# Splitting the first eight tiles of a fused LoRA kernel into parts of one and seven

## The chip, the cores and the metric

The kernel runs on one core of a Trainium2 chip. The metric is device time in microseconds (us) of one execution; the kernel before takes 124.86 us, the median of three runs (124.82 to 125.03). A profile, taken in an execution of its own, shows what each engine and each DMA queue did in it.

## The reference

A low-rank update is added to every row of x:

```python
"x": (16, 512, 768) f32, "A": (768, 16) f32, "B": (16, 768) f32, "scale": 0.5
lora = np.matmul(np.matmul(x, A), B)
return (x + scale * lora).astype(np.float32)
```

That is 8192 rows of 768 floats. They are read once and written once, 25.2 MB each way; A and B are 48 KB each.

## The kernel before

The 8192 rows are cut into 64 tiles of 128 rows, one row of a tile on each of the 128 partitions; a tile is 384 KB, 3 KB on each partition. Tiles are gathered in parts (`PARTS`, line 14): 8, 8, 16, 16 and 16 tiles. In a part of S tiles, partition p holds S rows that follow one another in memory (`memory`, line 88), so that a transfer of the whole part moves one piece of S x 3 KB for each partition. `LOADS` (line 98) and `STORES` (line 120) list the transfers as (part, first tile, tiles). The first part is read in two pieces, 2 tiles and then 6, the last in two of 8; the others in one. Every part is stored in one piece but the last, stored in two. The buffer `x_all` has room for 48 tiles (`ROOM`, line 57), so that the last 16 tiles are read into the places of the first 16, once these are stored.

The work runs in 8 groups of 8 tiles (`GROUP`, `NG`), two halves of 4 tiles in each. For each half ScalarE or GpSimd casts the x tiles to f16 (`narrowed`, line 168, the copy is L178), VectorE transposes them in 32x32 blocks (`turned`, L235), TensorE multiplies with A, which was laid out in blocks beforehand (`projected`, L263). ScalarE scales the small product and lays it out (L222), TensorE multiplies with B (`raised`, L280), for two tiles at a time, and VectorE adds the result to x in place (`summed`, L240). The addition that ends a group which is the last of a store raises the semaphore `s_sum`.

Every DMA is issued by SyncE (SP), on one queue, in an order written out by hand in `on_sync` (line 127): loads 0 and 1; A (L143) and B (L147), each after a memset by GpSimd; loads 2, 3 and 4. Then SP waits for the first low-rank product, issues store 0 as soon as the first group is added and store 1 as the second is (`store`, line 132, the wait at L133, the issue L138). Then it waits until store 0 has landed (line 159) and issues load 5, and for store 1 (line 161) and issues load 6; both fill places that these stores have emptied. At last it issues stores 2 to 5, each as its groups are added. A transfer of 128 partitions is spread over the core's 16 DMA engines; its completion adds up to 16 on a semaphore. `narrowed` waits for each load that its four tiles touch; for tiles 0 to 3 these are loads 0 and 1. GpSimd waits at the end (line 314) for the last four stores. `store` also gives TensorE the last `s_free` of a group, which on other groups the addition gives itself.

Of the kernel before, what the change touches and what calls it, by code (L numbers as in the profile page):

```python
# [10 lines left out]

PARTS = [8, 8, 16, 16, 16]


GROUP = 8
# [7 lines left out]
def kernel(  # L25
# [8 lines left out]
    nc = tc.nc  # L34
# [9 lines left out]
    NC = D // 64  # L44
    NG = sum(PARTS) // GROUP
    PAIRS = GROUP // 2
    assert sum(PARTS) * P == T and NG * GROUP == sum(PARTS)
    sc = float(scale)


    def sb(name, shape, dtype):
        return nc.alloc_sbuf_tensor(name, shape, dtype).ap()
# [3 lines left out]

    ROOM = sum(PARTS[:-1])
    x_all = sb("x_sb", [P, ROOM, D], fp32)
# [17 lines left out]
    def sem(name):  # L76
        return tc.alloc_semaphore(name)
# [3 lines left out]
    where = []  # L81
    tok = 0
    for i, S in enumerate(PARTS):
        parts.append(tok)
# [3 lines left out]
    def memory(t2, i, s, n):  # L88
        S = PARTS[i]
        return t2[ds(parts[i], S * P), :].rearrange("(p s) d -> p s d", s=S)[:, ds(s, n), :]  # L90

    def held(i, s, n):
        return tiles(where.index((i, s)), n)

    def tiles(t, n):
        return x_all[:, ds(t % ROOM, n), :]

    LOADS = [
        (0, 0, 2), (0, 2, 6), (1, 0, 8), (2, 0, 16), (3, 0, 16), (4, 0, 8), (4, 8, 8)
    ]  # L100
    s_load = [sem(f"s_load{k}") for k in range(len(LOADS))]

# [12 lines left out]
    s_free = [sem(f"s_free{p}") for p in range(PAIRS)]  # L115
    s_sum = sem("s_sum")
    s_out0, s_out1, s_out = sem("s_out0"), sem("s_out1"), sem("s_out")

    MMS = 2 * NC
    STORES = [(0, 0, 8), (1, 0, 8), (2, 0, 16), (3, 0, 16), (4, 0, 8), (4, 8, 8)]  # L120

    STORED = [where.index((i, s + n - 1)) // GROUP for i, s, n in STORES]

    section = ExitStack()
    section.enter_context(tc.tile_critical(no_gpsimd_drain=True))  # L125
# [1 line left out]
    def on_sync(e):  # L127
        def load(k):
            ld = LOADS[k]
            e.dma_start(out=held(*ld), in_=memory(x2, *ld)).then_inc(s_load[k], 16)  # L130

        def store(k, done):
            st = STORES[k]  # L133
            e.wait_ge(s_sum, k + 1)
            if STORED[k] + 1 < NG:

                e.sem_inc(s_free[PAIRS - 1], 1)
            e.dma_start(out=memory(out2, *st), in_=held(*st)).then_inc(done, 16)  # L138

        load(0)  # L140
        load(1)
        e.wait_ge(s_ready, 1)
        e.dma_start(  # L143
            out=a_rows[0 : NC * APART : APART, :], in_=A.rearrange("(c e) r -> c (e r)", e=64)
        ).then_inc(s_a, 16)
        e.wait_ge(s_brows, 1)
        e.dma_start(out=b_rows[0 : R * APART : APART, :], in_=B).then_inc(s_b, 16)  # L147
        for k in range(2, len(LOADS) - 2):
            load(k)

        e.sem_inc(s_spread, 1)
        for p, n in ((0, 1), (2, 2), (3, 2)):
            e.sem_inc(s_free[p], n)

        e.wait_ge(s_lora, 1)
        e.sem_inc(s_free[1], 1)
        store(0, s_out0)
        store(1, s_out1)
        e.wait_ge(s_out0, 16)
        load(len(LOADS) - 2)  # L160
        e.wait_ge(s_out1, 16)
        load(len(LOADS) - 1)
        for k in range(2, len(STORES)):
            store(k, s_out)

    here = set()
# [58 lines left out]
    def on_vector(e):  # L225
# [11 lines left out]
        def summed(g, p):  # L237
            xs = tiles(g * GROUP + 2 * p, 2)
            e.wait_ge(s_lora, (g + 1) * PAIRS + p + 1)
            ins = e.tensor_tensor(out=xs, in0=xs, in1=lora[p % 2], op=mybir.AluOpType.add)  # L240
            if p + 1 == PAIRS and g in STORED:
                ins.then_inc(s_sum, 1)
# [12 lines left out]
    def on_tensor(e):  # L255
# [49 lines left out]
        for p in range(PAIRS):  # L305
            raised(p)

    on_sync(nc.sync)
    on_gpsimd(nc.gpsimd)
    on_scalar(nc.scalar)  # L310
    on_vector(nc.vector)
    on_tensor(nc.tensor)

    nc.gpsimd.wait_ge(s_out, (len(STORES) - 2) * 16)
    section.close()


# [33 lines left out]
```

## Time and profile before

| what | before |
|---|---|
| median of 3 runs | 124.86 us |
| profiled execution, its own time | 125.2 us |
| span of that execution | 123.4 us |
| busy: TensorE, VectorE, ScalarE, GpSimd | 58.3, 82.5, 38.7, 27.3 us |
| DMA | 50.43 MB in 1928 packets, 409 GB/s over the span |
| load 0 (768 KB) from issue to landing | 4.7 us |
| load 1 (2304 KB) from issue to landing | 10.4 us |
| store 0 (3072 KB): issue, time to landing | 36.38 us, 19.4 us |
| last addition ends, last store is issued | 105.8 us |

The span goes from the first to the last instruction of the profiled execution; the profiled execution's own time is 1.8 us longer, and lies 0.34 us above the median. A packet is one contiguous piece that one DMA engine moved; a packet of 4 bytes at the end of a transfer on each engine raises its semaphore. "Busy" is the time in which an engine executes; "landing" is the time at which a transfer's semaphore is full.

### The profile page before, as it was taken

How to read it: one execution, taken by the hardware profiler on the slowest of the kernel's cores; microseconds unless marked ns; L12 is line 12 of the kernel's file. 1: busy time of each engine (PE TensorE's matmuls, PEld its weight loads, DVE VectorE, ACT ScalarE, POOL GpSimd, SP SyncE). 2: the span in 40 equal slices, each digit the busy share in tenths (PEclk: the TensorE clock that was granted, in tenths of full speed). 3: DMA queues.
4: the chain of work that ended last, by engine and by line, in shares of the span. 5: the costliest groups of instructions: out<-in, count | busy, mean ns of one | idle time of the engine just before them, and what ended most of it. 6: DMA issues, size and time to landing. Idle time of an engine off the chain costs nothing.

```text
span 123.4 us, 1313 instructions
## 1 busy us (share of the span) xinstructions
PE 58.3 (47%) x530; PEld 39.2 (32%) x530; DVE 82.5 (67%) x49; ACT 38.7 (31%) x43; POOL 27.3 (22%) x25
## 2 busy tenths in 40 slices
PE   0000249948565994844854775576484452000000
PEld 0000028736352862523614534255253311000000
DVE  0000555059985999999999999999999889200000
ACT  0001992760094085264083072353400400000000
POOL 7500660071035008005203501700800000000000
PEclk9999999999855599999999999999999999555555
DMA  3999996997999898999999999899989989899980
GB/s 66 422 430 372 430 574 287 510 478 335 462 494 398 382 510 358 398 446 430 430 454 390 446 446 502 382 414 478 462 351 478 446 382 446 382 446 414 438 366 8
DMA packets 1928, 50.43 MB, mean 409 GB/s; under 512 B 236, under 2 KB 236, under 8 KB 392
## 3 DMA queue, kind: packets, MB, share of 16 engines
q1 hardware_dynamic: 1928, 50.43, 96.1%
HBM read 25.26 MB, written 25.17 MB: 409 GB/s over the span
## 4 chain that ended last, share of the span: by engine, by line
DVE 54%; PE 13%; DMA 8%; ACT 5%; issue 4%; SPq 0%; ACTq 0%
DVE x_sb L240 38%; DVE xh L235 16%; DMA x_sb<-in_x_dram 8%; PE ps_yt L263 7%; PE lora_ps L280 6%; ACT xh L178 2%; ACT y_bd L222 1%; ACT L178 1%; ACT b_mm L214 1%; SPq L130 0%; SPq L346 0%; SPq L125 0%; ACTq L173 0%
## 5 line engine op out<-in xcount | busy, mean ns | idle before, releaser
L240 DVE TENSOR_TENSOR x_sb<-x_sb,lora_ps 128x1536 f32<-128x1536 f32 x32 | 54.1, 1732 | 3.2 <-PE lora_ps L280 3.2
L280 PE MATMUL lora_ps<-b_mm,y_bd 128*128 128x512 f16 (+1 forms) x144 | 30.6, 352 | 24.2 <-ACT y_bd L222 10.0
L178 ACT CAST xh<-x_sb 128x3072 f16<-128x3072 f32 x9 | 24.8, 2752 | 29.4 <-PE ps_yt L263 22.3
L235 DVE STREAM_TRANSPOSE xh<-xh 128x1536 f32<-128x1536 f32 x16 | 28.2, 1765 | 8.0 <-ACT xh L178 8.0
L263 PE MATMUL ps_yt<-xh,w_bd 128*128 128x128 f16 x384 | 28.2, 235 | 7.5 <-DVE xh L235 7.5
L178 POOL CAST xh<-x_sb 128x3072 f16<-128x3072 f32 x7 | 19.2, 2746 | 52.6 <-PE ps_yt L263 52.6
L263 PEld LDWEIGHTS ps_yt<-xh,w_bd 128*128 128x128 f16 x384 | 26.0, 105 | 12.7 <-issue 12.3
L280 PEld LDWEIGHTS lora_ps<-b_mm,y_bd 128*128 128x128 f16 x144 | 13.1, 103 | 37.7 <-issue 20.9
L222 ACT ACTIVATE y_bd<-ps_yt 32x256 f16<-32x256 f32 x32 | 12.0, 374 | 18.1 <-PE ps_yt L263 17.8
L227 DVE STREAM_TRANSPOSE a_t<-a_rows 96x1024 f32<-96x1024 f32 x1 | 1.9, 1930 | 12.1 <-DMA a_rows<-in_A_dram 12.1
L292 PE MATMUL lora_ps<-b_half,pick 128*128 128x512 f16 (+1 forms) x2 | 0.8, 504 | 13.4 <-POOL b_half L194 13.4
L178 ACT ACT_TABLE_LOAD x1 | 1.3, 1283 | 11.9 <-DMA x_sb<-in_x_dram 11.9
L292 PEld LDWEIGHTS lora_ps<-b_half,pick 128*128 128x128 f16 x2 | 0.1, 103 | 13.4 <-issue 13.4
L194 POOL CAST b_half<-b_rows 128x768 f16<-128x768 f32 x1 | 0.8, 822 | 7.6 <-DMA b_rows<-in_B_dram 7.6
L204 POOL COPY w_bd<-w_one 32x384 f16<-32x384 f16 x4 | 2.0, 500 | 0.2
L198 POOL CAST w_one<-a_t 32x128 f16<-32x128 f32 x3 | 1.2, 390 | 1.0 <-DVE a_t L227 0.8
L185 POOL MEMSET w_bd<- 128x1536 f32 x1 | 1.4, 1378 | 0.0
L182 POOL MEMSET a_rows<- 96x1024 f32 x1 | 0.9, 948 | 0.5 <-SPq L125 0.5
L214 ACT CAST b_mm<-lora_ps 128x768 f16<-128x768 f32 x1 | 0.8, 798 | 0.0
L183 POOL MEMSET b_rows<- 128x768 f32 x1 | 0.7, 734 | 0.0
L186 POOL MEMSET y_bd<- 128x512 f32 x1 | 0.5, 522 | 0.0
L188 POOL TENSOR_SCALAR_AFFINE_SELECT pick<-pick 128x128 f16<-128x128 f16 x1 | 0.3, 306 | 0.0
(5 smaller groups left out, 0.6 us busy)
## 6 DMA issues: line engine op xcount, KB each, us to landing
x_sb<-in_x_dram SPq DMA_DIRECT2D x2, 6144.0 KB, 36.8
out_dram<-x_sb SPq DMA_DIRECT2D x4, 3072.0 KB, 16.5
out_dram<-x_sb SPq DMA_DIRECT2D x2, 6144.0 KB, 22.0
x_sb<-in_x_dram SPq DMA_DIRECT2D x3, 3072.0 KB, 14.7
x_sb<-in_x_dram SPq DMA_DIRECT2D x1, 2304.0 KB, 10.4
x_sb<-in_x_dram SPq DMA_DIRECT2D x1, 768.0 KB, 4.7
a_rows<-in_A_dram SPq DMA_DIRECT2D x1, 48.0 KB
b_rows<-in_B_dram SPq DMA_DIRECT2D x1, 48.0 KB, 9.4
```

The source lines that it names most:

```text
L178: last = copy(out=xh[h][:, ds(k, n), :], in_=tiles(t + k, n))
L182: e.memset(a_rows[0 : NC * APART], 0.0).then_inc(s_ready, 1)
L185: e.memset(w_bd.rearrange("p c k m -> p (c k m)").bitcast(fp32), 0.0)
L198: e.tensor_copy(out=w_one[:, ds(b * EACH, EACH), :, :], in_=a_t[ds(b * Q, Q)].rearrange("i k r (c n) -> i c k r n", n=APART)[..., 0],).the ...
L204: e.tensor_copy(out=w_bd[ds(b * Q, Q), :, :, ds(b * Q, R)], in_=w_one).then_inc(s_w, 1)
L214: e.copy(out=b_mm, in_=lora[0][:, 0, :]).then_inc(s_bm, 1)
L222: last = e.mul(out=y_bd[q, :, q], in_=y_ps[q, :, :], mul=sc)
L227: e.transpose(out=a_t[0 : NC * APART].rearrange("i k r c -> i (k r) c"), in_=a_rows[0 : NC * APART].rearrange("c (i k r) -> c (k r) i", k= ...
L235: e.transpose(out=v, in_=v).then_inc(s_turned[h], 1)
L240: ins = e.tensor_tensor(out=xs, in0=xs, in1=lora[p % 2], op=mybir.AluOpType.add)
L263: mm = e.matmul(y_ps[:, ds(h * SUB, SUB), :], w_bd[:, c, k, :], xv[:, :, c, :, k], start=(m == 0), stop=(m == MMS - 1),)
L280: mms.append(e.matmul(t[:, k, ds(n0, w)], y_bd[:, 2 * p + k, :], b_mm[:, ds(n0, w)], start=True, stop=True,))
```

## The change

The first 8 tiles become two parts, of 1 and of 7 tiles, each read in one transfer. The part of 7 is stored first, right behind it the 1, both after the first group's additions; both count up `s_out0`, and load 5 waits for the 32 of both. `store` waits on `s_sum`, and gives `s_free`, only for the first store that ends in a group. The memory rows that a partition holds change with it: one row of the first 128, and 7 that follow one another of the next 896. In memory, the first load went over pieces of 6 KB that are 24 KB apart, the second over pieces of 18 KB; now they are pieces of 3 KB and of 21 KB that follow one another. The number of transfers goes from 15 to 16.

```diff
-PARTS = [8, 8, 16, 16, 16]
+PARTS = [1, 7, 8, 16, 16, 16]
...
     LOADS = [
-        (0, 0, 2), (0, 2, 6), (1, 0, 8), (2, 0, 16), (3, 0, 16), (4, 0, 8), (4, 8, 8)
+        (0, 0, 1), (1, 0, 7), (2, 0, 8), (3, 0, 16), (4, 0, 16), (5, 0, 8), (5, 8, 8)
     ]
...
-    STORES = [(0, 0, 8), (1, 0, 8), (2, 0, 16), (3, 0, 16), (4, 0, 8), (4, 8, 8)]
-
-    STORED = [where.index((i, s + n - 1)) // GROUP for i, s, n in STORES]
+    STORES = [(1, 0, 7), (0, 0, 1), (2, 0, 8), (3, 0, 16), (4, 0, 16), (5, 0, 8), (5, 8, 8)]
+
+    ENDED = [where.index((i, s + n - 1)) // GROUP for i, s, n in STORES]
+    STORED = list(dict.fromkeys(ENDED))
...
         def store(k, done):
             st = STORES[k]
-            e.wait_ge(s_sum, k + 1)
-            if STORED[k] + 1 < NG:
-
-                e.sem_inc(s_free[PAIRS - 1], 1)
+            if k == 0 or ENDED[k] != ENDED[k - 1]:
+                e.wait_ge(s_sum, STORED.index(ENDED[k]) + 1)
+                if ENDED[k] + 1 < NG:
+
+                    e.sem_inc(s_free[PAIRS - 1], 1)
             e.dma_start(out=memory(out2, *st), in_=held(*st)).then_inc(done, 16)
...
         store(0, s_out0)
-        store(1, s_out1)
-        e.wait_ge(s_out0, 16)
+        store(1, s_out0)
+        store(2, s_out1)
+        e.wait_ge(s_out0, 32)
         load(len(LOADS) - 2)
         e.wait_ge(s_out1, 16)
         load(len(LOADS) - 1)
-        for k in range(2, len(STORES)):
+        for k in range(3, len(STORES)):
             store(k, s_out)
...
-    nc.gpsimd.wait_ge(s_out, (len(STORES) - 2) * 16)
+    nc.gpsimd.wait_ge(s_out, (len(STORES) - 3) * 16)
```

## The prediction

> **What bounds the kernel now.** I read the page from the DMA rows outward, because the list of costly groups alone would point to VectorE: DVE is busy 67% of the span, and the chain that ended last is 54% DVE.
>
> ```profile
> DMA  3999996997999898999999999899989989899980
> q1 hardware_dynamic: 1928, 50.43, 96.1%
> DVE 54%; PE 13%; DMA 8%; ACT 5%; issue 4%; SPq 0%; ACTq 0%
> ```
>
> The first row is the share of the 16 DMA engines in use, in 40 slices: full from the second slice to the last but one. The second says that one queue moved 50.43 MB and that its packets took 96.1% of 16 engines' span. The chain's shares add up to 84%, and in order of time it stops with VectorE's last addition at 105.8 us, while the span ends at 123.4; what fills the rest is the stores. The DMA view cut to 12 to 120 us settles it:
>
> ```profile
> DMA packets 1543, 46.50 MB, mean 431 GB/s; under 512 B 163, under 2 KB 163, under 8 KB 163
> q1 hardware_dynamic: 1543, 46.50, 100.0%
> ```
>
> 100.0% for 108 us: the queue never runs dry. So the kernel lasts as long as its packets do, plus about 2 us before the first (share 0.06 in the windows view from 0 to 2 us) and about 3 us behind the last (0.06 from 120 to 122). A second question is whether SP always issues the next transfer before the queue is empty. The timeline of SP (start us, duration us, line) gives the issues:
>
> ```profile
> 0.97 0.85 SPq L130 DMA_DIRECT2D x_sb<-in_x_dram  x2
> 3.47 1.74 SPq L130 DMA_DIRECT2D x_sb<-in_x_dram  x3
> 36.38 12.33 SPq L138 DMA_DIRECT2D out_dram<-x_sb  x2
> 55.78 7.63 SPq L130 DMA_DIRECT2D x_sb<-in_x_dram  x2
> 68.33 37.83 SPq L138 DMA_DIRECT2D out_dram<-x_sb  x4
> ```
>
> A merged row covers several issues; asked one by one, the DMA view gives each one's time to landing. The last early load lands at 48.4 (issued near 4.7, 43.7 later, the longest landing), and store 0 was issued at 36.38: 12.0 us of cover. Store 0 lands at 55.8 (19.4 after issue), store 1 at 63.1 (48.38 + 14.7), the two late loads at 70.4 and 77.8 (55.78 + 14.6, 63.07 + 14.7), the next stores at 92.8 (68.33 + 24.5), 107.7 (88.27 + 19.4), 114.9 (98.25 + 16.7) and 122.2 (105.83 + 16.4). Each issue against the landing ahead of it: cover of 7.3 us for both late loads, 9.5 for the store at 68.33, 4.5 at 88.27, 9.5 at 98.25, 9.1 at 105.83. The smallest is 4.5 us.
>
> **The change part by part.** Compute first: the order of instructions on PE, DVE, ACT and POOL stays as it was; only SP gets one DMA more.
>
> *Price of a packet.* The trace's records of single packets have one length for each size, nearly without exception: 3 KB (3072 B) 121 ns, 6 KB 234, 18 KB 686, 24 KB 912, 48 KB 1815. From 24 to 48 KB it is 903 ns for 24,576 B, 36.7 ns per 1000 B, which leaves about 8 ns per packet; 3072 B by that line are 121, as seen, and 21 KB (21,504 B) come to 799. A completion packet of 4 B takes 9 ns. Each transfer of 128 rows is 8 packets on each of 16 engines.
>
> *The two first loads.* Before: 8 x 234 + 8 x 686 = 7.36 us on each engine. After: 8 x 121 + 8 x 799 = 7.36 us. Nothing. ScalarE's first cast takes tiles 0 to 3, which span both loads before and after, so its start (table load at 11.88, on load 1, issued at 1.35 with 10.4 to landing) stays; that load 0 alone lands sooner helps nobody. If the first load is now so short that the second is not ready behind it, a gap opens: the first's packets began 1.0 us after its issue (0.97 to 1.97) and 1.7 us after it at the latest (2.65); the second is issued at 1.35, so ready from 2.4 to 3.1; the first now needs 0.97 us of packets, and the very first of each engine was some 0.5 us longer than 234 ns. It ends at 2.9 at the earliest and mostly after 3.3. No gap.
>
> *The first stores.* Before: 8 x 912 + 9 = 7.31 us. After, 8 x 799 + 9 and 8 x 121 + 9 = 7.38 us: **+0.07 us**, in a full queue, so it reaches the end whole. SP's own issue of the second store (0.34 us) comes right behind the first, at 36.7, and next on SP is the wait for the second group at 48.4: 11 us of cover.
>
> *The wait for both stores.* Load 5 now waits for two completions in one semaphore. They come 0.07 us later than the one of before; queued behind that wait on SP are load 6 and the stores from 68.33 on, all with at least 4.5 us of cover. If that cover were gone, the same 0.07 us would be paid once more.
>
> *Order.* POOL's last wait counts the same four stores. The 1 and 7 tiles lie where the 8 lay, so the wrap of the last 16 tiles onto the first stays.
>
> *Unknown: 3 KB packets in a row.* No row shows eight in a row, nor a store of 3 KB. Nearest are the 16 of 3 KB that load B: 11 at 121 to 133 ns, the others up to 219, mean 141. So one 1-tile transfer costs between nothing and 8 x 98 ns = 0.78 us more than the line says, 0.16 at the mean. And behind the two small loads of A and B the first 24 KB packet on most engines took near 1340 ns for 912: a stall of **0.43 us**, where the completions came 0.13 to 0.17 us apart. Behind load 0 (1.9 us of packets) load 1's first packets were mostly 686, no stall. A 1-tile transfer lies between, 0.97 us from completion to completion. Its nearest row is that of load 0: half as long, against a seventh. I take no stall and the line's 121 ns; both upper ends go to the range.
>
> *Below nothing.* Load 0's packets took 328 ns in the mean for 234: 8 x 94 = 0.75 us on each engine are lost as the traffic starts. If that went with the bytes of the first load, half would go: -0.37 us. Much of it is the first packet's own wait, though, which stays.
>
> *A rule that speaks against the change.* The Trainium skill, "DMA: Bandwidth & Descriptors", section "Anatomy of one DMA — SWDGE (gpsimd) path", gives a DMA (measured on those that GpSimd issues) a fixed cost of about 2.0 us, mostly the receipt of the last write; by that an added DMA would cost an estimated 2 us if nothing hid it, 126.9 us in all. Here store 1 lands 7.3 us behind store 0 and its packets alone take 7.3: the next transfer runs under the receipt.
>
> *Sum.* The profiled execution took 125.2 us, its span 123.4. With +0.07 it is 125.27; the median of the runs, 124.86, is 0.34 lower, so **124.93 us**. A measurement of this kernel tells about 0.2% (0.25 us) from no change, and this is 0.06%.
>
> **The rivals.**
>
> *Short transfers stall the queue (slower).* Place: the 1-tile store and the packet behind it. It decides if completions 0.97 us apart are still too close. Price: the 0.43 us stall of A and B, with 0.16 us for each of the two 3 KB transfers at B's mean: +0.50 to +0.82 in all, 125.4 to 125.7 us. For it: the stall stands in the trace. Against: it came with gaps of 0.17 us, and a stall that makes up a fixed delay (0.17 + 0.43 = 0.6 us) would be over after 0.97. With every 3 KB packet at its worst, and a stall behind both, it is +2.5 us, 127.4; this needs the worst of 16 packets 16 times running.
>
> *The start loses less (faster).* Half of load 0's 0.75 us goes: 124.56 us. For it: the lost time is spread over several packets of an engine, not only its first. Against: load 1 then is the one to start, with more packets left in the slow stretch.
>
> *A fixed cost shows (slower).* If the added store had its own start and receipt in the open, it would cost the 1.0 us from issue to first packet and some 0.4 us from last packet to landing: 126.3 us. Against: 100.0% from 12 to 120 us over 8 such seams.
>
> *It does not do what it says.* Were the 128 rows of the 1-tile part joined into fewer, longer packets, as they lie in one piece in memory, the time would be that of before, 124.86. The 8-tile part, in one piece too, was 128 packets of 24 KB, so I expect 128 of 3 KB.
>
> **How the numbers follow.** Forecast, with the joined rows: 0.57, from 124.75 to 125.1. Stall 0.25. Less lost at the start 0.15. Fixed cost 0.03. So faster by over 0.2% 0.15, within 0.2% 0.57, slower 0.28. The range reaches over the first two rivals: low 124.55, high 125.7; left out are the fixed cost, the worst packets, and what lies below the half of the start.
>
> **What would show it.** Small packets: under 8 KB from 392 to near 536 (128 of 3 KB in the store, 16 completions; the first load's 128 stay under 8 KB). From 12 to 120 us still 100.0%. The seven tiles land some 1 us before the one; the wait ahead of load 5 ends at 55.8 to 55.9. Last addition still at 105.8, last store's landing at 122.3. Wrong would be: a first 24 KB packet behind the 1-tile store well above 912 ns, 3 KB packets well above 121, or a DMA share under 9 tenths near 55 us.

## The result and the profile after

The changed kernel is slower: 125.28 us median (124.97 to 126.52, 22 runs) against 124.96 (124.72 to 125.43, 22 runs), a ratio of 1.0042 with an interval of 1.0026 to 1.0058. Measured twice more it came to 1.0021 (1.0007 to 1.0035) and 1.0032 (1.0015 to 1.0050). The medians lie 0.30 to 0.33 us apart in all three; the first ratio is larger because 8 of its 22 runs took more than 125.55 us. Two runs of e2 below (126.91 and 127.13 us) lie over 1.5% above the fastest of their kernel and are left out of its median and ratio.

The rows of the page of the changed kernel that answer to those shown of before, in the same order:

```profile
DMA  3999999899799697999999999799899989899980
q1 hardware_dynamic: 2072, 50.43, 96.3%
DVE 50%; DMA 24%; ACT 5%; PE 3%; SPq 2%; POOL 1%; issue 1%; POOLq 0%
```

2072 packets for 1928, as many more as eight on each engine and one more completion make. The queue is still full, and between 12 and 120 us, by the DMA view, its share is 100.2%:

```profile
DMA packets 1683, 46.38 MB, mean 429 GB/s; under 512 B 180, under 2 KB 180, under 8 KB 308
q1 hardware_dynamic: 1683, 46.38, 100.2%
```

SP issues as planned (start us, duration us, line), three stores merged in the row at 34.25, the late loads at 55.79:

```profile
0.97 0.86 SPq L131 DMA_DIRECT2D x_sb<-in_x_dram  x2
3.47 1.59 SPq L131 DMA_DIRECT2D x_sb<-in_x_dram  x3
34.25 13.90 SPq L140 DMA_DIRECT2D out_dram<-x_sb  x3
55.79 7.66 SPq L131 DMA_DIRECT2D x_sb<-in_x_dram  x2
67.77 37.84 SPq L140 DMA_DIRECT2D out_dram<-x_sb  x4
```

So nothing ran dry, and yet some time went. Where it went is seen when a window's GB/s is divided by its DMA share. Both count a packet where it begins, so the quotient is the rate of the packets while they run. These are the windows of the first profile of before (columns: window, its length, busy time and number of instructions of PE, PEld, DVE, ACT and POOL, granted clock, DMA share, GB/s):

```profile
12.00:44.00 32.00, 21.76 (x166) 15.57 (x167) 21.58 (x13) 16.20 (x15) 9.48 (x10) 0.84 1.03 444
44.00:50.00 6.00, 3.93 (x38) 2.40 (x35) 6.00 (x5) 3.92 (x5) 2.75 (x1) 1.00 0.85 365
50.00:74.00 24.00, 15.46 (x160) 10.25 (x160) 24.00 (x15) 10.80 (x11) 5.49 (x2) 1.00 1.01 434
```

and of the changed kernel in its third profile (run e9_after_third below):

```profile
12.00:44.00 32.00, 20.65 (x178) 14.59 (x179) 22.23 (x14) 17.10 (x15) 8.94 (x10) 0.95 1.02 442
44.00:50.00 6.00, 4.01 (x52) 3.02 (x48) 6.00 (x5) 2.17 (x5) 2.75 (x1) 1.00 0.90 325
50.00:74.00 24.00, 14.62 (x148) 9.40 (x147) 24.00 (x16) 11.26 (x11) 5.50 (x2) 1.00 1.01 433
```

Before: 444/1.03 = 431, 365/0.85 = 429, 434/1.01 = 430. Changed: 433, then 325/0.90 = 361, then 429. From 44 to 50 us the early loads end and the first stores begin; I call it **the seam**. The DMA engines there are busy but move a sixth less. In the first profile of the changed kernel it is less marked, 353/0.90 = 392:

```profile
44.00:50.00 6.00, 3.84 (x43) 2.59 (x42) 6.00 (x5) 3.39 (x5) 2.75 (x1) 1.00 0.90 353
```

The records of single packets show which packets are slow: the last 48 KB packet of load 4 on every engine, 2.3 to 2.9 us long in that third profile for 1.815.

The gain ahead of it shows in the time to landing of load 1 in the DMA view, the last column. Before:

```profile
x_sb<-in_x_dram SPq DMA_DIRECT2D x1, 2304.0 KB, 10.4
...
x_sb<-in_x_dram SPq DMA_DIRECT2D x1, 6144.0 KB, 43.7
```

Changed, third profile:

```profile
x_sb<-in_x_dram SPq DMA_DIRECT2D x1, 2688.0 KB, 9.6
...
x_sb<-in_x_dram SPq DMA_DIRECT2D x1, 6144.0 KB, 43.6
```

Load 1 lands 0.8 us sooner after an issue at the same time, load 4 (6144 KB) no longer does. These are the last of 16 engines. The engine in the middle (median of the 16 completions) scatters less; its landings, as means of two profiles of before and three of the changed kernel, in us:

| landing | before | changed | difference |
|---|---|---|---|
| load 1 | 10.88 | 10.44 | -0.44 |
| load 3 | 33.22 | 32.74 | -0.48 |
| load 4 | 47.78 | 47.93 | +0.16 |
| first store or stores | 55.07 | 55.28 | +0.21 |
| last store | 120.49 | 120.78 | +0.29 |

In these means half a microsecond is gained at the start, 0.64 us is lost between load 3 and load 4, and 0.13 us behind it. The last row is as large as the difference of the medians of the runs (+0.30 to +0.33), but it can't be taken as its proof, for two reasons. The landing of load 4 differs less between the kernels than within them: 47.88 and 47.68 before, 47.75, 48.08 and 47.97 changed. And an execution ends with its last engine, not with the middle one: its time is some 3.0 us more than the last landing of the last store in every profile (3.1 in e6). That landing came at 122.20 and 121.88 before and at 121.98, 122.31 and 122.21 changed, 0.13 us later in the mean; the five executions themselves took 125.20 and 124.87, and 124.98, 125.30 and 125.20 us, also 0.13 us apart. The loss at the seam is there in every profile of the changed kernel; that it is what makes up the 0.3 us of the medians is not shown by so few profiles.

### The profile page after: what moved, and what is told of

It reads as the page before. It is cut to its first block, busy times and chain, and to the rows that moved or that the text cites. A ratio compares the mean times of both kernels' runs of the same rounds, so it can differ in the third digit from the quotient of the medians.

```text
span 123.2 us, 1314 instructions
## 1 busy us (share of the span) xinstructions
PE 55.6 (45%) x530; PEld 36.9 (30%) x530; DVE 82.5 (67%) x49; ACT 38.7 (31%) x43; POOL 27.3 (22%) x25
## 2 busy tenths in 40 slices
DMA packets 2072, 50.43 MB, mean 409 GB/s; under 512 B 252, under 2 KB 252, under 8 KB 536
## 3 DMA queue, kind: packets, MB, share of 16 engines
q1 hardware_dynamic: 2072, 50.43, 96.3%
## 4 chain that ended last, share of the span: by engine, by line
DVE 50%; DMA 24%; ACT 5%; PE 3%; SPq 2%; POOL 1%; issue 1%; POOLq 0%
DVE x_sb L243 35%; DMA x_sb<-in_x_dram 24%; DVE xh L238 15%; ACT y_bd L225 2%; ACT xh L181 2%; PE lora_ps L283 2%; PE ps_yt L266 1%; POOL a_rows L185 1%; SPq L145 1%; SPq L131 0%; SPq L149 0%; POOLq L349 0%; SPq L126 0%
## 5 line engine op out<-in xcount | busy, mean ns | idle before, releaser
L283 PE MATMUL lora_ps<-b_mm,y_bd 128*128 128x512 f16 (+1 forms) x144 | 30.1, 348 | 26.9 <-ACT y_bd L225 15.3
L266 PE MATMUL ps_yt<-xh,w_bd 128*128 128x128 f16 x384 | 25.9, 224 | 7.4 <-DVE xh L238 7.4
L266 PEld LDWEIGHTS ps_yt<-xh,w_bd 128*128 128x128 f16 x384 | 23.9, 99 | 12.7 <-issue 12.3
```

Of the source, the lines that this page charges most:

```text
L266: mm = e.matmul(y_ps[:, ds(h * SUB, SUB), :], w_bd[:, c, k, :], xv[:, :, c, :, k], start=(m == 0), stop=(m == MMS - 1),)
L283: mms.append(e.matmul(t[:, k, ds(n0, w)], y_bd[:, 2 * p + k, :], b_mm[:, ds(n0, w)], start=True, stop=True,))
```

## The experiments

In the profiles I read three numbers besides the time: the landing of load 3 on the middle engine; the loss at the seam, which is the length of all packets that begin from 40 to 48 us beyond the usual length of their size, divided by 16 engines; and the time from load 4's landing to that of the stores of the first eight tiles. Load 3 and load 4 are in every kernel the two early loads of 16 tiles; in e11 and e12, where the second is cut in two, the landing is that of its second piece. The diffs show only the changed part of a long line.

| kernel | load 3 us | seam loss us | load 4 us | first stores us |
|---|---|---|---|---|
| before, first profile | 33.34 | 0.02 | 47.88 | 7.27 |
| before again, e4 | 33.11 | 0.09 | 47.68 | 7.33 |
| e8, stores 6, 1, 1 | 33.07 | 0.16 | 47.68 | 7.38 |
| e2, loads 1, 7 alone | 32.95 | 0.39 | 47.73 | 7.30 |
| e3, stores 7, 1 alone | 32.95 | 0.42 | 47.77 | 7.33 |
| changed, first profile | 32.87 | 0.49 | 47.75 | 7.35 |
| e6, one load of 8 | 32.83 | 0.47 | 47.69 | 7.33 |
| e1, changed | 32.72 | 0.92 | 48.08 | 7.35 |
| e7, one tile stored first | 32.72 | 0.77 | 47.92 | 7.35 |
| e10, the same | 32.65 | 0.84 | 47.87 | 7.36 |
| e9, changed | 32.64 | 0.90 | 47.97 | 7.35 |
| e11, changed, late store | 32.74 | 0.05 | 47.35 | 7.32 |
| e12, before, late store | 33.29 | 0.05 | 47.89 | 7.28 |
| e5, changed, store held | 32.57 | 0.01 | 47.10 | - |

**e1: the changed kernel again** (no edit).

> The changed kernel as it is, to see which of its lost time comes back. In its first profile every engine's last 48 KB packet of load 4 (the packets that began at 45.0 to 45.7 us) took 2.0 to 2.5 us for 1.815, about 0.5 us lost per engine at the seam from loads to stores; before had nothing there. Theory S (the added store upsets that seam, now that two stores are queued behind the loads): the stretch of about 0.5 us is there again, median 1.002 to 1.006 of before. Theory N (the seam's stretch is a chance of that one execution): under 0.1 us this time, and the runs scatter from 124.9 to 126.5 for a reason that the seam doesn't show.

125.24 us against 124.91; seam loss 0.92. The stretch of the last packets was there again, and larger, so theory N falls for the changed kernel. Its window gives 314/0.87 = 361 GB/s at the seam:

```profile
44.00:50.00 6.00, 3.83 (x47) 2.97 (x48) 6.00 (x5) 1.93 (x5) 2.75 (x1) 1.00 0.87 314
```

**e2: only the loads.**

```diff
-        (0, 0, 2), (0, 2, 6), (1, 0, 8),
+        (0, 0, 1), (0, 1, 7), (1, 0, 8),
```

> Parts and stores as before; the first part is read as 1 and 7 tiles in place of 2 and 6. Only the sizes of the first two loads change. Theory S: the loss came from the store, so this is no slower than before, 0.996 to 1.001 (load 1 lands up to 0.6 us sooner, as it did in the changed kernel: 11.2 for 11.8 us). Theory L (3 KB packets at the start are what scatters): slower by 0.2 to 0.6%, with single runs up to 126.5.

124.98 us against 124.91, ratio 1.0018 (0.9995 to 1.0040). Not clear of no change. The stretch is there (0.39) without any added store, so theory S, that the added store makes it, falls. Theory L, that small first packets scatter the runs, is neither shown nor excluded by this interval.

**e3: only the stores** (the changed `store`, with parts and loads of before).

```diff
-    STORES = [(0, 0, 8), (1, 0, 8),
+    STORES = [(0, 1, 7), (0, 0, 1), (1, 0, 8),
```

> Parts and loads as before; the first part is stored as 7 tiles and then 1, with rows of 21 KB and 3 KB that lie 24 KB apart in memory. One store more than before. Theory S: the whole loss, 1.002 to 1.006 of before, with the stretch before the first store in the profile. Theory L: no loss, 1.000 to 1.001. If both parts alone are within 0.1% of before, it is the layout: rows of 3 KB and 21 KB that follow one another.

125.09 us, 1.0011 (0.9997 to 1.0025), seam loss 0.42. Inconclusive in time: the halves alone come to +0.07 and +0.18 us in the median and neither is clear of nothing. The stretch came with either half, in one profile each. But the loads of e3 are those of before, and here load 3 landed at 32.95 for 33.11 and 33.34: so early an arrival, with the stretch, does not need the new loads.

**e4: before again** (no edit).

> The kernel before as it is, for a second profile of it. Theory S: no stretch at the seam from loads to the first store (last 48 KB packets near 1815 ns, as in the first profile). Theory N: the stretch comes and goes here too, anything from 0 to 0.5 us.

124.87 us, seam loss 0.09, most of it on the three engines that came first to the seam. As theory S had it for before; but with e2 beside it, what goes with the loss is not the added store. In the table it goes with the landing of load 3: the sooner the loads come, the more is lost, and load 4 lands at 47.7 to 48.1 whatever was gained. I formed two theories from that: the turn (T: loads with a store queued behind them are held) and the early arrival by itself (A).

**e5: no store in the queue behind the loads.**

```diff
+        e.wait_ge(s_load[len(LOADS) - 3], 16)
         store(0, s_out0)
```

> The changed kernel, in which SP waits for the last early load (load 4, about 47.7 to 48.1 us) before it issues the first store: no store stands queued behind the loads. The queue runs dry for 1 to 2 us there, which is the price of looking. Theory T (the turn: the last 48 KB packets of load 4 are held because a store follows them in the queue): they take about 1.815 us, no more than 0.1 us lost per engine before 48 us, where three profiles of changed kernels lost 0.39 to 0.92. Theory A (the engines arrive at the end of the loads early and together, whatever follows): the stretch of 0.3 to 0.9 us stays.

129.91 us, seam loss 0.01, load 4 lands at 47.10, 0.87 us ahead of e9. As T had it. But the price was far above the queue's dry spell, for a reason that I had overlooked: `store` also hands TensorE the buffer of the next group, behind my wait. VectorE stood for 8.5 us at just that time (lines are shifted by one in this kernel):

```profile
49.50 1.75 DVE L244 TENSOR_TENSOR x_sb<-x_sb,lora_ps 128x1536 f32<-128x1536 f32 x1 [8.46 <-PE lora_ps L284]
```

So it also fits a third theory, C: the sums that run beside the transfers hold them.

**e6: one first load of 8 tiles** (so `load(1)` and the loop behind it move up by one).

```diff
-        (0, 0, 2), (0, 2, 6), (1, 0, 8),
+        (0, 0, 8), (1, 0, 8),
```

> The kernel before with its first part read in one transfer of 8 tiles: packets of 24 KB from the start, one transfer less. Theory of the first load's size (smaller first packets lose less at the start, and the seam takes it back): loss per engine before 9.5 us at least that of before, 0.7 to 0.8 us (3 KB first packets: 0.36 to 0.64), and little stretch at the seam, below 0.2 us; time 0.999 to 1.002 of before. Rival: the start's loss does not follow the size of the first packets; then it is anywhere from 0.3 to 0.8.

124.95 us, 1.0010 (0.9999 to 1.0022). The start lost 0.69 us (before 0.69 and 0.78), as expected; the seam 0.47, which I had put below 0.2. It stands in its place in the table by the landing of load 3, not by the size of its first packets.

**e7: the one tile stored first.**

```diff
-    STORES = [(1, 0, 7), (0, 0, 1),
+    STORES = [(0, 0, 1), (1, 0, 7),
```

> The changed kernel with the one tile stored ahead of the seven: the 3 KB packets then come right at the seam from loads to stores, where eight small packets leave little in flight. If the order matters, 0.1 to 0.5 us slower or faster than the changed kernel (125.24); if it is only the number of packets and the reading at the start, the same within 0.1 us: 1.002 to 1.003 of before.

124.94 us, 1.0004 (0.9993 to 1.0016). Its eight small packets on each engine took 121 ns each, right at the seam. The time is below the changed kernel's 125.24 of e1, so I ran both side by side (e10). With a seam loss of 0.77 it is not clear of before here: the loss at the seam alone does not tell how slow a kernel is.

**e8: two stores more** (the changed `store`, parts and loads of before; 48 in the wait for `s_out0`).

```diff
-    STORES = [(0, 0, 8), (1, 0, 8),
+    STORES = [(0, 2, 6), (0, 0, 1), (0, 1, 1), (1, 0, 8),
```

> Loads and parts as before; the first part is stored as 6 tiles, then 1, then 1: two stores more than before, where the kernel with stores of 7 and 1 had one more and came to 125.09 against 124.91. If an added store costs what its packets do (0.07 us), this is +0.15 us, 125.05. If each added store costs 0.18 us as that run's median seemed to say, +0.36 us, 125.27. The landing of the last of the three small stores, seen from the landing of load 4, tells it with less scatter: 7.3 us before, +0.07 or +0.18 for each.

124.88 us, 1.0003 (0.9993 to 1.0013). The first stores took 7.38 us: one store 7.27 to 7.33 in the four profiles above (before, e4, e2, e6), mean 7.30; two 7.33 to 7.36, mean 7.35; three 7.38. So an added store costs some 0.04 us, and not 0.18.

**e9: the changed kernel a third time** (no edit), **and e10: e7 again**, on one chip.

> The changed kernel once more, beside the two below on one chip: 1.002 to 1.004 of before, loss at the seam before 48 us 0.4 to 0.9 us, load 1 landing near 10.4 us (median of the engines).

> The changed kernel with the one tile stored ahead of the seven, a second time, now beside the changed kernel itself. It came to 1.0004 of before, though its profile showed the same early start and the same stretch at the seam (0.77 us) as the changed kernel. If the order of the two stores matters, it is again below the changed kernel by 0.1 to 0.4 us. If that was scatter between calls, the two are within 0.1 us of each other.

e9: 125.20 us, 1.0032 (1.0015 to 1.0050); e10: 125.06 us, 1.0020 (1.0002 to 1.0038). Seam losses 0.90 and 0.84. The intervals overlap, and in the profiles the two orders behave alike; whether the order matters by 0.1 us stays open.

**e11 and e12: a late first store**, in the changed kernel and in before. The last early load is cut into 13 and 3 tiles; `store` waits for the 13 behind the release of TensorE, so that the sums go on.

```diff
-(4, 0, 16), (5, 0, 8),
+(4, 0, 13), (4, 13, 3), (5, 0, 8),
...
                     e.sem_inc(s_free[PAIRS - 1], 1)
+            if k == 0:
+                e.wait_ge(s_load[len(LOADS) - 4], 16)
             e.dma_start(out=memory(out2, *st), in_=held(*st)).then_inc(done, 16)
```

> The changed kernel with the last early load cut into 13 and 3 tiles; SP waits for the 13 before it issues the first store, and TensorE is released as before, so that the sums go on, which they did not in the run that held the store until the whole load. The store then comes into the queue only some 1 to 2 us before the loads end. Theory T (a store that stands behind the loads holds their last packets): the last 48 KB or 39 KB and 9 KB packets are hardly stretched, under 0.2 us lost before 48 us, and the time is 0.3 to 0.5 us below the changed kernel, at or below before. Theory C (the sums running beside it hold them): the stretch of 0.4 to 0.9 us stays.

> The same late first store in the kernel before (first load of 2 tiles, one store of 8). Its profiles lost 0.02 and 0.09 us at the seam, so there is little to win: 0.998 to 1.002 of before. If it wins as much as the changed kernel does, it is not the seam that sets the two kernels apart.

The first store of e11 was issued at 44.89 for 34.01 to 35.51 in the changed kernels, and at the seam the packets nearly kept their rate, 436/1.03 = 423 GB/s, while VectorE was busy for all 6 us:

```profile
44.89 2.41 SPq L142 DMA_DIRECT2D out_dram<-x_sb  x3
```

```profile
44.00:50.00 6.00, 4.01 (x53) 3.12 (x51) 6.00 (x4) 2.22 (x5) 2.75 (x1) 1.00 1.03 436
```

The loss is 0.05, and load 4 lands 0.62 us sooner than in e9. The sums went on, so C alone falls, and so does A, as load 3 had landed early (32.74). That bears out T: the early store in the queue is needed for the hold. e11 by itself leaves another reading, as its last packets are 9 KB long and no longer 48; in e5 they were 48 KB, and were not held either. But a store queued early is not enough: in before it stands there as well (issued at 36.38 and, in e4, at 34.55), with 0.02 and 0.09 lost.

e11 came to 125.10 us, 1.0028 (1.0004 to 1.0052), not the 0.3 to 0.5 us below the changed kernel that I expected. Some 0.14 us is the price of the cut itself: 39 KB and 9 KB took 1479 and 352 ns, 16 more than 48 KB in one, eight times, and there is one completion more. By its profile it lost 0.45 us from 74 to 78 us, at the second seam from loads to stores, where the changed kernel lost 0.08 to 0.12, and 0.23 from 48 to 74 us for 0.03 or 0.04. Against e9 it spared 0.85 us at the first seam and lost 0.54 more behind it; its last store landed 0.27 us sooner on the middle engine. e12, which had nothing to spare at the first seam, lost 0.90 from 74 to 78 us and 0.56 from 48 to 74 and was slower, 125.43 us, 1.0050 (1.0028 to 1.0071). So the hold at the seam can be taken away, but that this makes the changed kernel faster is not shown: the intervals of e9 and e11 overlap. No version beat before.

## Why the prediction was right or wrong, point by point

The measured 125.28 us lies in the range of 124.55 to 125.7, but on the side that had 0.28, and not at the likeliest case (124.75 to 125.1). That the range holds it is luck: its upper end was built on stalls behind the 3 KB transfers, which did not come, and the loss that did come has no term in the sum.

*The bound.* Right: the DMA queue sets the end, every issue kept its cover, and the last addition ends at 98.50 + 6.75 = 105.3 us for the 105.8 expected, without bearing on the end.

*The price of the packets and of the added store.* Right in kind: 121 ns and 799 ns are the medians of 272 and 256 packets (the 16 of B among the first), and one store more costs about 0.04 us where +0.07 was forecast. The rule of the Trainium skill, "DMA: Bandwidth & Descriptors", section "Anatomy of one DMA — SWDGE (gpsimd) path", by which the prediction gave 126.9 us had nothing hidden its fixed cost, does not show here, in a full queue.

*The two first loads: "Nothing."* Here the sum failed first. Load 1 landed 0.44 us sooner. The loss before 9.5 us fell from 0.69 to 0.78 us per engine to 0.36 to 0.53, so the rival "the start loses less" had the place right and nearly the size (0.37 us). Its rule, that the loss goes with the bytes of the first load, is not borne out: e6, with 8 tiles first, lost 0.69, no more than before with 2, and e2, with 1 tile first, lost 0.64. What made the start's loss smaller stays open.

*"In a full queue, so it reaches the end whole."* This was said of the added store's +0.07 us, which comes behind the seam, and there it is not contradicted: the first stores took 0.05 us longer in the means. But the whole sum rests on the same idea, that what changes in a full queue is carried to the end unchanged, and this is the step that failed. I took a share of 100.0% for packets at full rate, and gave load 4's last packets, which the change does not touch, no term. The share counts a held packet as busy; 0.49 to 0.92 us per engine hid in it at the seam, against 0.02 and 0.09 before. So a gain ahead of the seam did not reach the end: of the 0.48 us at load 3 nothing was left at load 4, which in the means landed 0.16 us later than before. None of the signs that I had named looked at these packets.

*The rival "short transfers stall the queue".* Its sum, 125.4 to 125.7 us, lies just above the median, and the place was wrong: of the 24 KB packets at and behind the 1-tile store none took more than 993 ns for 912 in the three profiles, and e8 with two such stores was no slower than before.

*The change does what it says.* Yes: 128 packets of 3 KB each way.

What is shown: the loss at the seam goes with how early the loads come (table), also where neither half of the change is in the kernel (e6, 0.47), and goes away at that place if the store is issued late (e5 and e11). What is not: why a store that waits behind loads holds their last packets, why that depends on a time near 47.7 us, and why losses turn up later when this one is spared. The 0.30 us of the medians fits the middle engine's landings and is not proven by them. Nor was one of the changed kernel's long runs profiled: in the seven sets with a first load of 1 tile 17 of 92 runs took more than 125.55 us, in before and in e3, e6 and e8 none of 148. But the first load alone does not make them: e12, with 2 tiles first and a late store, had 4 of 9, and e1 and e7, with 1 tile, had none of 24. The cause of this tail, which lifts the first ratio to 1.0042, is open. The one profile of so long a run, e12 at 125.85 us, has its losses at the later seams.

## What to carry to other kernels

A queue that is busy all the time can still lose time: divide GB/s by the busy share, window by window, and look hardest where reading turns to writing. A gain at the start of such a queue is worth nothing until it is seen behind the next seam. Read the last engine as well as the middle one before a difference in a profile is taken for that of the times. An added store that splits 384 KB off a larger one in a full queue cost 0.04 us, no more than the 0.07 us by which its packets are longer in sum.

## What was not expected of the hardware

The last packet of a load was held by up to 1.11 us (2.93 us for 48 KB, 1.815 alone), on all 16 engines at once, when a store had stood in the same queue for 9 us or more (e9; in e4, with a store queued as early, 0.09 us per engine was lost in all); only 0.05 us per engine was lost when the store was issued some 2.5 us ahead of the loads' end (e11). In the eleven profiles with the store queued early, load 4 landed within 0.4 us (47.68 to 48.08 on the middle engine), though load 3 had landed over a spread of 0.7 us (32.64 to 33.34).
